# Pairing float32 products of two heads, and new durations in the list schedule of a two-layer hybrid encoder

## The chip, the cores and the metric

The kernel runs on one core of one Trainium2 chip. The time is the device time of one execution in microseconds (us). TensorE is called PE here, its weight loads PEld, VectorE DVE, ScalarE ACT, GpSimd POOL, as the profile names them.

## The reference

The kernel computes a trunk of two layers on 512 tokens of width 1024. Each layer is a half-step SwiGLU feed-forward, a mixing block and a second half-step SwiGLU:

```python
for l in range(DEPTH):
    x = x + 0.5 * swiglu(rms_norm(x, norm_ffn1[l]), ffn1_w_in[l], ffn1_w_out[l])
    h = rms_norm(x, norm_mix[l])
    proj = h @ w_in[l]                      # RWKV-7 | band attention | memory attention
    y_rwkv, v_first = rwkv7_time_mix(p_rwkv, h, ...)
    y_att = chunked_rel_attention(aq, ak, av, att_rel_bias[l])
    y_mem = memory_attention(mq, mk, mv)
    merged = (g_rwkv * (y_rwkv @ w_branch_rwkv[l]) + g_att * (y_att @ w_branch_att[l])
              + g_mem * (y_mem @ w_branch_mem[l]))
    x = x + merged @ w_out[l]
    x = x + 0.5 * swiglu(rms_norm(x, norm_ffn2[l]), ffn2_w_in[l], ffn2_w_out[l])
```

RWKV-7 has 8 heads of 64, with a delta-rule state scan over time; the band attention has 8 heads of 64 and sees all earlier chunks of 64 tokens (512 tokens are 8 chunks, so the band is causal by chunk); the memory attention has 4 heads of 128 over 256 memory tokens.

## The kernel before

**Large products.** All products with weights run in float16 as three terms (high by high, high by low, low by high), each 128 rows by 128 columns by 512 moving columns as a rule. The weights come in float32 by DMA and are split into two float16 halves by ACT and DVE (`load_w`). They fill most of the PE's time: `g<-hh,wh` and its likes in the trace.

**Small products.** The three mixers do their inner products in float32. [...] Heads go in pairs `p` of two heads of 64, one on partitions 0 to 63 and one on partitions 64 to 127 (`H2`; `W2` is the same in the other order), four pairs in a layer.

- `rwkv()` works through the four pairs one after the other. For each pair it computes decay and in-context rate from two products of 64 rows by 128 columns by 512 (`s<-xwa,lw` in the trace; lora products below), then the pair's matrices, a triangular inverse by levels (`each`, 16 products of 64x64x64), and a scan over 8 chunks. In one chunk of the scan the steps depend on each other: the product `xps<-ar,gx`, a copy to `cx`, the product `xps<-cx,tt`, scaled copies to `vu` (`kk` and `ta` in the trace), the product `xps<-kk,kb` and `xps<-ta,be`, and two writes of the next state `z` (`ar<-xps,aw,czc`). The chunk's output `yp` takes four products (two for each head, summed in PSUM), on which nothing in the scan waits.
- `band()` works through the four pairs of attention heads. For each block `b` of 128 queries and each head `u`, `soft(b, u)` makes one score product of 64 rows by 128 columns by `nk` = 128(b+1) keys (`as<-ak,aq`), adds the bias, takes the maximum, exponentials, and scales; `turn` transposes the result into PSUM (`as<-con,sc`) and copies it out (`pt`). Both take their PSUM tile from `a_ps()`, a ring of two banks. `soft` of the next head is called ahead of `turn` of the one before.
- `mem_att()` follows `band()` on the same ring, one of the four memory heads after the other.
- `branch` makes gates and output products for the three mixers, band first, RWKV last. Its sums `acc` lie where the attention's tiles were, so they wait for the end of `mem_att()`.

The lora products, the levels and the transposes of `rwkv()` take PSUM from `s_ps()`, also a ring of two banks.

**What sets the order.** The program isn't issued as written. Recorders note every call with its tiles; `Plan.run` then makes a list schedule: it plays the five engines with estimated durations (`Plan.cost`) and hop times between engines (`HOPS`, `Plan.hop`), takes on each engine the ready operation with the longest path to the end (`key`), and issues the calls in that order. All instructions of PE therefore carry one line, L538, where the calls are made. Operations of a `plan.block()` stay together. For PE, an operation that isn't float16 adds 0.45 of its duration to a debt, and above 0.5 us of debt a float16 product goes first. Where the play finds PE idle for more than 0.4 us it puts in products of zeros (`xps<-wt`) to keep the clock. The estimated PE durations before are these:

```python
if lhs.off.size <= CH // 2:
    return 0.015 + n / 1200
if lhs.off.size <= CH:
    return 0.0255 + n / 1200
return 0.01 + n / 600
```

`n` is the number of moving columns; a block's duration is the sum over its products.

Of the kernel before, what the change touches and what calls it, by code (L numbers as in the profile page):

```python
# [16 lines left out]
P = 128  # L17
# [8 lines left out]
CH = 64  # L26
# [184 lines left out]
class Op:  # L211
    __slots__ = ("eng", "calls", "us", "deps", "succ", "tail", "n", "left", "ready", "end", "bytes", "cols", "big", "phase", "sum", "lift")
# [15 lines left out]
class Plan:  # L228
    HOPS = {"PE": (0.2, 0.2), "S": (0.14, 0.27), "V": (0.14, 0.21), "G": (0.06, 0.3), "D": (0.5, 0.5)}
# [36 lines left out]
    def block(self):  # L266
        plan = self

        class Block:
            def __enter__(s):  # L270
                plan.cur = plan.new("PE")

            def __exit__(s, *a):
                plan.cur = None

        return Block()
# [59 lines left out]
    def cost(self, o, eng, name, out, ins, k):  # L336
# [5 lines left out]
        if eng == "PE":  # L342
            n = out.off.size
            if n <= 2:
                return 0.16
            if name == "transpose":
                o.cols += n
                return 0.005 + n / 1200
            rhs, lhs = k["rhs"], k["lhsT"]
            if rhs.root.dt == F16:  # L350
                o.cols += n
                o.big = True
                o.sum = id(out.root), int(out.off.flat[0])
                return 0.0028 + n / 2400
            o.cols += 2 * n * (rhs.p1 - rhs.p0) / P
            if lhs.off.size <= CH // 2:
                return 0.015 + n / 1200
            if lhs.off.size <= CH:
                return 0.0255 + n / 1200
            return 0.01 + n / 600  # L360
# [3 lines left out]
        if eng == "V":  # L364
            if name == "memset" or name == "reciprocal" and n <= 8:
                return 0.075
            if name in ("tensor_scalar", "tensor_copy") and not psum and out.root.dt != I32:
                return 0.07 + n / 1920 + 0.06 * aps
            return 0.07 + n / 960 + 0.06 * aps
        if eng == "S":  # L370
            return (0.06 if psum else 0.1) + n / 1200 + 0.09 * ((aps > 0) + ("accum_out" in k))
# [168 lines left out]
    def hop(self, a, b):  # L540
# [3 lines left out]
        if a.eng == b.eng:  # L544
            return 0.12 if a.eng == "V" else 0.0
# [10 lines left out]
def trunk(tc: tile.TileContext, i: dict, out: bass.AP, dbg: dict | None = None, depth: int = DEPTH):  # L556
# [414 lines left out]
    def mixing(l, pieces, kst):  # L971
# [106 lines left out]
        def band():  # L1078
            for p in range(NP):
# [22 lines left out]
                def soft(b, u):  # L1102
                    nk = (b + 1) * P
                    h = H2[u]
                    ps = a_ps()
                    PE.matmul(ps[:, :nk], lhsT=q_[h, b * P:(b + 1) * P], rhs=k_[h, 0:nk], start=True, stop=True)
# [23 lines left out]
                for b in range(4):  # L1130
                    for u in range(2):
                        pend.append(soft(b, u))
                        if len(pend) > 1:
                            turn(*pend.pop(0))
# [100 lines left out]
        def rwkv():  # L1235
            for p in range(NP):
# [17 lines left out]
                ps = s_ps()  # L1254
                PE.matmul(ps, lhsT=glob["lw"][0:CH, cs], rhs=glob["xwa"][0:CH, :], start=True, stop=True)
# [3 lines left out]
                ps = s_ps()  # L1259
                PE.matmul(ps, lhsT=glob["lw"][CH:P, cs], rhs=glob["xwa"][CH:P, :], start=True, stop=True)  # L1260
                ta = tr("ta")
                S.activation(ta, ps, AF.Tanh, scale=0.5, bias=lv["a0"][:, p:p + 1])
# [114 lines left out]
                for c in range(NCH):  # L1377
# [26 lines left out]
                    with plan.block():  # L1404
                        for u, h in enumerate(H2):
                            o, w = yp[h, c * CH:(c + 1) * CH], W2[u]
                            PE.matmul(o, lhsT=gx[:, c, u, CH:2 * CH], rhs=vz[:, c, u, :], start=True, stop=False)
                            PE.matmul(o, lhsT=g1[w, c, :], rhs=vu[u][w, c, :], start=False, stop=True)
# [269 lines left out]
```

## Time and profile before

| | |
|---|---|
| median of 3 runs | 2773.04 us (2770.26 to 2778.02) |
| profiled execution, its own time | 2773.73 us |
| its span, first to last instruction | 2771.9 us |
| DVE busy | 1626.2 us (59%) |
| ACT busy | 1538.0 us (55%) |
| granted PE clock, mean | 0.999 of 2.4 GHz |

The profile gives busy time as the union of the intervals of an engine's instructions. For PE these overlap: a float16 product of 512 columns shows some 0.38 us, and the next one starts 0.22 us after it. What a product costs PE is therefore read from the distance between starts (to the start of what follows), not from its own length.

### The profile page before, as it was taken

The numbers are of one execution on the slowest core, as the hardware profiler recorded it, in microseconds if no ns is written. First come the engines' busy times: TensorE is split into PE (matmuls) and PEld (weight loads), VectorE is DVE, ScalarE is ACT, GpSimd is POOL, SyncE is SP. The second block draws the span as 40 slices with busy tenths as digits, with TensorE's granted clock in tenths as the row PEclk, the third lists the DMA queues.
The fourth block names the chain that finished last, engine by engine and source line by source line (L and its number), as shares of the span: only waits on it lengthen the run. The fifth ranks groups of instructions, "written<-read, shape, count | busy, mean of one in ns | idle before, by whom it ended". The sixth has DMA issues, their size and how long they took to land. (4 is left out here: it accounts for less than half of the span.)

```text
span 2771.9 us, 45458 instructions
## 1 busy us (share of the span) xinstructions
PE 2745.1 (99%) x18153; PEld 1496.6 (54%) x18153; DVE 1626.2 (59%) x4391; ACT 1538.0 (55%) x2543; POOL 111.1 (4%) x285
## 2 busy tenths in 40 slices
PE   9999999999999999999999999999999999999999
PEld 6444486565645456444564444765655454654445
DVE  6344486777766676354463544777776666743543
ACT  6556475565645566565455654655655445655652
POOL 0000000000000000000000000000000000000000
PEclk9999999999999999999999999999999999999999
DMA  4222341111121223222222223311212112232332
GB/s 169 105 93 103 122 140 69 51 61 45 52 83 70 85 98 115 95 104 99 99 107 105 93 106 118 129 52 42 70 35 75 67 54 92 92 114 100 107 106 77
DMA packets 47157, 249.36 MB, mean 90 GB/s; under 512 B 5312, under 2 KB 10688, under 8 KB 23648
## 3 DMA queue, kind: packets, MB, share of 16 engines
q1 hardware_dynamic: 46944, 246.45, 25.2%
q8 instruction: 142, 2.33, 0.3%
q14 instruction: 71, 0.58, 0.1%
HBM read 239.09 MB, written 7.34 MB: 89 GB/s over the span
## 5 line engine op out<-in xcount | busy, mean ns | idle before, releaser
L538 PEld LDWEIGHTS <-wh 128*128 128x128 f16 x10920 | 1047.6, 98 | 1008.0 <-issue 26.8
L538 PE MATMUL g<-hh,wh 128*128 128x512 f16 (+1 forms) x3216 | 987.0, 367 | 0.4 <-DVE k L538 0.4
L538 ACT ACTIVATE wh<-wr,qs 128x1024 f16<-128x1024 f32 (+2 forms) x478 | 484.0, 1050 | 222.5 <-PE g L538 114.3
L538 ACT ACTIVATE junk<-wr 128x2048 uint8<-128x2048 f32 (+2 forms) x239 | 412.9, 1727 | 332.9 <-DMA wr<-ffn_in 144.3
L538 PE MATMUL g<-hl,wh 128*128 128x512 f16 (+1 forms) x1608 | 588.9, 366 | 0.0
L538 DVE SCALAR_TENSOR_TENSOR wh<-wr,qs,wh 128x1024 f16<-128x1024 f32 (+2 forms) x478 | 545.2, 1168 | 43.8 <-ACT wh L538 42.9
L538 PE MATMUL as<-hh,wh 128*128 128x512 f16 (+1 forms) x1536 | 443.3, 361 | 0.0
L538 PE MATMUL as<-hl,wh 128*128 128x512 f16 (+1 forms) x768 | 277.4, 361 | 0.0
L538 PE MATMUL as<-ab,wh 128*128 128x512 f16 (+1 forms) x1224 | 234.7, 350 | 0.0
L538 PE MATMUL g<-ab,wh 128*128 128x512 f16 (+1 forms) x1224 | 234.5, 350 | 0.0
L538 POOL PARTITION_ALL_REDUCE ar<-wm x239 | 97.3, 407 | 2465.5 <-ACT junk L538 2313.6
L538 DVE SCALAR_TENSOR_TENSOR a<-as,md,sg 128x512 f32<-128x512 f32 x44 | 33.0, 750 | 213.3 <-PE as L538 210.0
L538 DVE SCALAR_TENSOR_TENSOR a<-g,md,sg 128x512 f32<-128x512 f32 x44 | 33.0, 750 | 212.9 <-PE g L538 202.7
L538 DVE SCALAR_TENSOR_TENSOR x<-g,md,x 128x512 f32<-128x512 f32 (+1 forms) x62 | 39.0, 628 | 115.8 <-PE g L538 115.8
L538 DVE SCALAR_TENSOR_TENSOR x<-as,md,x 128x512 f32<-128x512 f32 (+1 forms) x62 | 38.9, 628 | 115.8 <-PE as L538 115.8
L538 DVE TENSOR_SCALAR qt<-ar 128x1 int32<-128x1 int32 x253 | 37.6, 150 | 104.0 <-POOL ar L538 101.7
L538 ACT ACTIVATE sq<-x 128x256 f32<-128x256 f32 x96 | 37.0, 407 | 78.9 <-DVE x L538 50.6
L538 ACT ACTIVATE kk<-xps 64x64 f32<-64x64 f32 x64 | 14.0, 219 | 112.6 <-DVE ta L538 93.9
L538 ACT ACTIVATE ti<-s 64x256 f32<-64x256 f32 (+1 forms) x144 | 54.3, 378 | 28.2 <-PE s L538 18.3
L538 DVE SCALAR_TENSOR_TENSOR ab<-a,qs,ab 128x512 f16<-128x512 f32 x88 | 60.7, 746 | 10.3 <-ACT ab L538 10.3
L538 ACT ACTIVATE sg<-as,md 128x512 f32<-128x512 f32 x44 | 30.1, 684 | 56.2 <-PE as L538 56.2
L538 ACT ACTIVATE ab<-a,qs 128x512 f16<-128x512 f32 x88 | 55.9, 709 | 7.3 <-DVE qs L538 7.3
(345 smaller groups left out, 3133.4 us busy)
## 6 DMA issues: line engine op xcount, KB each, us to landing
wr<-ffn_in SPq DMA_DIRECT2D x88, 1024.0 KB, 4.8
wr<-ffn_outa SPq DMA_DIRECT2D x32, 1024.0 KB, 4.9
wr<-w_gate SPq DMA_DIRECT2D x24, 1024.0 KB, 4.9
wr<-w_in SPq DMA_DIRECT2D x22, 1024.0 KB, 4.9
wr<-ffn_outb SPq DMA_DIRECT2D x16, 768.0 KB, 4.3
wr<-w_branch SPq DMA_DIRECT2D x24, 512.0 KB, 3.5
wr<-mem_kv SPq DMA_DIRECT2D x8, 1024.0 KB, 4.9
wr<-w_out SPq DMA_DIRECT2D x8, 1024.0 KB, 4.8
```

What stands on the lines that cost most here:

```text
L538: f(*[x.real() if isinstance(x, View) else x for x in a], **{y: x.real() if isinstance(x, View) else x for y, x in k.items()})
```

## The change

The two score products of a block `b` are made together: a new function `scores` takes both banks of the ring and issues both heads' products in one `plan.block()`; `soft` gets its bank as an argument. The two lora products go into one block and take both banks of their ring at once. In the block of `yp` the order of the four products changes from head by head to both first products, then both second ones. In the planner, blocks of 2, 4 or 16 products of given shapes take a duration from the table `GROUPS`; products of up to 2 columns cost 0.2 instead of 0.16; a DVE operation whose input and output start at different partitions costs 0.11 more; and an ACT operation that depends on another of ACT is ready 0.12 us after it instead of at once. What is computed stays the same.

```diff
--- before.py
+++ after.py
@@ -209,7 +209,7 @@
 
 
 class Op:
-    __slots__ = ("eng", "calls", "us", "deps", "succ", "tail", "n", "left", "ready", "end", "bytes", "cols", "big", "phase", "sum", "lift")
+    __slots__ = ("eng", "calls", "us", "deps", "succ", "tail", "n", "left", "ready", "end", "bytes", "cols", "big", "phase", "sum", "lift", "form", "kind")
 
     def __init__(self, eng, n):
         self.eng, self.n = eng, n
@@ -226,6 +226,12 @@
 
 
 class Plan:
+
+    GROUPS = {
+        2: {(128, CH, CH): 0.266, (CH, CH, CH): 0.264, **{(CH, P, n): 0.212 + n * 0.001656 for n in (128, 256, 384, 512)}},
+        4: {(128, CH, CH): 0.5},
+        16: {(CH, CH, CH): 1.08},
+    }
     HOPS = {"PE": (0.2, 0.2), "S": (0.14, 0.27), "V": (0.14, 0.21), "G": (0.06, 0.3), "D": (0.5, 0.5)}
     SLACK = 0.04
     RATIO, DEBT = 0.45, 0.5
@@ -271,6 +277,9 @@
                 plan.cur = plan.new("PE")
 
             def __exit__(s, *a):
+                o = plan.cur
+                if len(o.calls) in plan.GROUPS and o.form in plan.GROUPS[len(o.calls)]:
+                    o.us = plan.GROUPS[len(o.calls)][o.form]
                 plan.cur = None
 
         return Block()
@@ -341,8 +350,9 @@
         n = max([v.off.size for v in ins + [out] if isinstance(v, View)])
         if eng == "PE":
             n = out.off.size
+            o.form = None
             if n <= 2:
-                return 0.16
+                return 0.2
             if name == "transpose":
                 o.cols += n
                 return 0.005 + n / 1200
@@ -353,6 +363,9 @@
                 o.sum = id(out.root), int(out.off.flat[0])
                 return 0.0028 + n / 2400
             o.cols += 2 * n * (rhs.p1 - rhs.p0) / P
+            if len(o.calls) == 1:
+                o.kind = (rhs.p1 - rhs.p0, lhs.off.size, n)
+            o.form = o.kind
             if lhs.off.size <= CH // 2:
                 return 0.015 + n / 1200
             if lhs.off.size <= CH:
@@ -362,11 +375,20 @@
         aps = sum(v.off.size == 1 and v is not out and n > 1 for v in vs)
         psum = any(v.root.pool.kw.get("space") == PSUM for v in ins)
         if eng == "V":
+            moved = 0.11 * bool(ins and isinstance(out, View) and ins[0].p0 != out.p0 and name != "memset")
+            return moved + self.cost_v(name, n, aps, psum, out)
+        return self.cost_s(eng, name, n, aps, psum, k)
+
+    @staticmethod
+    def cost_v(name, n, aps, psum, out):
             if name == "memset" or name == "reciprocal" and n <= 8:
                 return 0.075
             if name in ("tensor_scalar", "tensor_copy") and not psum and out.root.dt != I32:
                 return 0.07 + n / 1920 + 0.06 * aps
             return 0.07 + n / 960 + 0.06 * aps
+
+    @staticmethod
+    def cost_s(eng, name, n, aps, psum, k):
         if eng == "S":
             return (0.06 if psum else 0.1) + n / 1200 + 0.09 * ((aps > 0) + ("accum_out" in k))
         if name == "partition_all_reduce":
@@ -542,7 +564,7 @@
         if a.eng not in self.HOPS:
             return 0.0
         if a.eng == b.eng:
-            return 0.12 if a.eng == "V" else 0.0
+            return 0.12 if a.eng in "VS" else 0.0
         return self.HOPS[a.eng][b.eng == "PE"] + self.SLACK
 
     def key(self, o):
@@ -1099,11 +1121,16 @@
                     t = ta_("pt", [P, 1280], bufs=2)
                     pt.append([t[:, c0:c0 + T - b * P] for b, c0 in enumerate((0, 512, 896, 1152))])
 
-                def soft(b, u):
+                def scores(b):
                     nk = (b + 1) * P
-                    h = H2[u]
-                    ps = a_ps()
-                    PE.matmul(ps[:, :nk], lhsT=q_[h, b * P:(b + 1) * P], rhs=k_[h, 0:nk], start=True, stop=True)
+                    pss = [a_ps(), a_ps()]
+                    with plan.block():
+                        for ps, h in zip(pss, H2):
+                            PE.matmul(ps[:, :nk], lhsT=q_[h, b * P:(b + 1) * P], rhs=k_[h, 0:nk], start=True, stop=True)
+                    return pss
+
+                def soft(b, u, ps):
+                    nk = (b + 1) * P
                     sc = ta_("sc", bufs=3)
                     far = max(0, nk - 2 * P)
                     for c0, c1, bb in ((0, far, bias[:, u, 0:1].to_broadcast([P, far])), (far, nk, bias[:, u, 2 * P - (nk - far):2 * P])):
@@ -1128,8 +1155,9 @@
 
                 pend = []
                 for b in range(4):
+                    pss = scores(b)
                     for u in range(2):
-                        pend.append(soft(b, u))
+                        pend.append(soft(b, u, pss[u]))
                         if len(pend) > 1:
                             turn(*pend.pop(0))
                 turn(*pend.pop(0))
@@ -1251,15 +1279,15 @@
                 else:
                     D.dma_start(out=vfs[p], in_=v_)
 
-                ps = s_ps()
-                PE.matmul(ps, lhsT=glob["lw"][0:CH, cs], rhs=glob["xwa"][0:CH, :], start=True, stop=True)
+                ps, ps2 = s_ps(), s_ps()
+                with plan.block():
+                    PE.matmul(ps, lhsT=glob["lw"][0:CH, cs], rhs=glob["xwa"][0:CH, :], start=True, stop=True)
+                    PE.matmul(ps2, lhsT=glob["lw"][CH:P, cs], rhs=glob["xwa"][CH:P, :], start=True, stop=True)
                 tz = tr("w", bufs=3)
                 S.activation(tz, ps, AF.Tanh, scale=0.5, bias=lv["w0"][:, p:p + 1])
                 V.tensor_scalar(out=tz, in0=tz, scalar1=1.0, scalar2=None, op0=ALU.add)
-                ps = s_ps()
-                PE.matmul(ps, lhsT=glob["lw"][CH:P, cs], rhs=glob["xwa"][CH:P, :], start=True, stop=True)
                 ta = tr("ta")
-                S.activation(ta, ps, AF.Tanh, scale=0.5, bias=lv["a0"][:, p:p + 1])
+                S.activation(ta, ps2, AF.Tanh, scale=0.5, bias=lv["a0"][:, p:p + 1])
                 cu = tr("w", bufs=3)
                 V.tensor_tensor_scan(out=cu, data0=con[:, C_CM:C_CM + T], data1=tz, initial=0.0, op0=ALU.mult, op1=ALU.add)
 
@@ -1402,9 +1430,10 @@
                             else:
                                 S.activation(z, xp_[w, 2 * CH:3 * CH], AF.Copy, scale=aw[w, c:c + 1])
                     with plan.block():
-                        for u, h in enumerate(H2):
-                            o, w = yp[h, c * CH:(c + 1) * CH], W2[u]
+                        ys = [yp[h, c * CH:(c + 1) * CH] for h in H2]
+                        for u, o in enumerate(ys):
                             PE.matmul(o, lhsT=gx[:, c, u, CH:2 * CH], rhs=vz[:, c, u, :], start=True, stop=False)
+                        for u, (o, w) in enumerate(zip(ys, W2)):
                             PE.matmul(o, lhsT=g1[w, c, :], rhs=vu[u][w, c, :], start=False, stop=True)
```

## Rows read from the trace of the kernel before

**Rows 1.** The page's first part: busy us, share of the span and instructions of each engine.

```profile
PE 2745.1 (99%) x18153; PEld 1496.6 (54%) x18153; DVE 1626.2 (59%) x4391; ACT 1538.0 (55%) x2543; POOL 111.1 (4%) x285
```

**Rows 2.** Busy time of each engine by stretch: the mixing of the first layer, that of the second, and the stretches of `mem_att()` in each. Columns: stretch and its length in us, busy us and instructions of each engine, granted clock, DMA share, GB/s.

```profile
400.00:945.00 545.00, 535.72 (x4583) 307.12 (x4582) 384.01 (x1194) 297.99 (x613) 18.73 (x48) 1.00 0.19 64
1765.00:2323.00 558.00, 549.23 (x4630) 311.78 (x4628) 393.49 (x1196) 303.46 (x622) 19.74 (x48) 1.00 0.19 64
690.00:763.00 73.00, 71.37 (x691) 46.04 (x691) 54.00 (x160) 42.77 (x97) 1.71 (x5) 1.00 0.16 54
2055.00:2139.00 84.00, 81.33 (x721) 50.00 (x723) 63.01 (x181) 48.27 (x106) 1.45 (x5) 1.00 0.09 28
```

**Rows 3.** The groups of PE's instructions, with different shapes kept apart. After the count: busy us in all, mean ns of one record, idle us before them. A float32 product is two records.

```profile
L538 PE MATMUL yp<-ar,gx 128*64 128x64 f32 x256 | 40.3, 239 | 0.0
L538 PE MATMUL xps<-ar,gx 128*64 128x64 f32 x256 | 21.5, 246 | 0.0
L538 PE MATMUL yp<-kk,g 64*64 64x64 f32 x128 | 20.8, 242 | 0.0
L538 PE MATMUL yp<-ta,g 64*64 64x64 f32 x128 | 20.8, 242 | 0.0
L538 PE MATMUL xps<-cx,tt 64*64 64x64 f32 x256 | 21.2, 243 | 0.0
L538 PE MATMUL s<-ar,be 64*64 64x128 f32 x256 | 15.9, 273 | 0.1
L538 PE MATMUL as<-ak,aq 64*128 64x512 f32 x32 | 17.9, 640 | 0.3 <-DVE qt L538 0.3
L538 PE MATMUL as<-ak,aq 64*128 64x384 f32 x32 | 14.5, 535 | 0.0
L538 PE MATMUL as<-ak,aq 64*128 64x256 f32 x32 | 11.1, 428 | 0.0
L538 PE MATMUL as<-ak,aq 64*128 64x128 f32 x32 | 3.9, 322 | 0.0
L538 PE MATMUL s<-xwa,lw 64*128 64x512 f32 x32 | 15.7, 639 | 0.7 <-DVE w L538 0.6
```

**Rows 4.** The timeline of PE (start us, length us, what) around two lora products that already stand next to each other (4 records), and around a single one (2 records).

```profile
421.29 0.38 PE L538 MATMUL g<-hh,wh 128*128 128x512 f16 x1
421.60 1.13 PE L538 MATMUL s<-xwa,lw 64*128 64x512 f32 x4
422.67 0.39 PE L538 MATMUL g<-hh,wh 128*128 128x512 f16 x1
...
542.48 0.38 PE L538 MATMUL g<-hh,wh 128*128 128x512 f16 x1
542.78 1.12 PE L538 MATMUL s<-xwa,lw 64*128 64x512 f32 x2
543.84 0.39 PE L538 MATMUL g<-hh,wh 128*128 128x512 f16 x1
```

**Rows 5.** The timeline of PE in one chunk of the last scan of the first layer: the four products of `yp` (8 records), and the next chunk's first two products, which hold both heads.

```profile
904.20 0.28 PE L538 MATMUL yp<-ar,gx 128*64 128x64 f32 x2
904.41 0.33 PE L538 MATMUL yp<-kk,g 64*64 64x64 f32 x2
904.66 0.33 PE L538 MATMUL yp<-ar,gx 128*64 128x64 f32 x2
904.92 0.33 PE L538 MATMUL yp<-ta,g 64*64 64x64 f32 x2
905.18 0.82 PE L538 MATMUL as<-ym,wh 128*128 128x512 f16 x3
905.93 0.34 PE L538 MATMUL xps<-ar,gx 128*64 128x64 f32 x4
906.20 0.82 PE L538 MATMUL as<-ym,wh 128*128 128x512 f16 x3
906.95 0.33 PE L538 MATMUL xps<-cx,tt 64*64 64x64 f32 x4
907.21 0.39 PE L538 MATMUL g<-hh,wh 128*128 128x512 f16 x1
```

**Rows 6.** The timeline of DVE in the same chunk: the two writes of `z` that the product at 905.93 needs.

```profile
904.48 0.58 DVE L538 SCALAR_TENSOR_TENSOR ar<-xps,aw,czc 64x64 f32<-64x64 f32 x2 [0.75 <-ACT junk L538]
```

**Rows 7.** The end of the first layer's RWKV branch: DVE's first and second finished half of `yr`, and PE's first product that reads it.

```profile
932.76 0.75 DVE L538 SCALAR_TENSOR_TENSOR yr<-yr,qs,yr 128x512 f16<-128x512 f32 x1 [0.54 <-ACT yr L538]
...
945.14 0.81 PE L538 MATMUL as<-yr,wh 128*128 128x512 f16 x3
```

**Rows 8.** Two groups of the band attention, of DVE (the bias of a score) and ACT (copies of transposes), with the idle time before them and what ended it.

```profile
L538 DVE SCALAR_TENSOR_TENSOR sc<-as,rq,bias 128x256 f32<-128x256 f32 x64 | 29.5, 478 | 15.2 <-PE as L538 14.5
L538 ACT ACTIVATE pt<-as 128x128 f32<-128x128 f32 x160 | 33.8, 284 | 28.4 <-PE as L538 27.8
```

**Rows 9.** Products of zeros in the second layer's `mem_att()`, as its end comes (PE's timeline).

```profile
2130.90 1.81 PE L538 MATMUL xps<-wt 128*128 128x320 f16 x12 [0.51 <-DVE cx L538]
...
2137.58 0.85 PE L538 MATMUL xps<-wt 128*128 128x320 f16 x5
```

**Rows 10.** First score products of blocks b = 2 and b = 3 in the third pair of the first layer (PE's timeline).

```profile
612.09 0.91 PE L538 MATMUL as<-ak,aq 64*128 64x384 f32 x2
...
617.83 1.12 PE L538 MATMUL as<-ak,aq 64*128 64x512 f32 x2
```

## The prediction, made before the changed kernel was built or run

> **What bounds the kernel now.** I read the engine totals first: PE is busy for 2745.1 of 2771.9 us, DVE and ACT for less than 60% [rows 1]. The span is a sequence of PE instructions with hardly a hole, so a microsecond less of PE's work can be worth a microsecond, provided that no other chain takes over where the work went. Then I cut the span into stages. All that is paired lies in the two mixing stretches, 545 and 558 us long, in which PE is idle for 545.00 - 535.72 = 9.3 and 558.00 - 549.23 = 8.8 us [rows 2]. The feed-forward stretches are float16 products alone, and the change leaves these as they are.
>
> Third, I asked whether a chain beside PE ends at the same moment. In the scan, the second write of `z` ends at 904.48 + 0.58 = 905.06, and the product that needs it starts at 905.93 [rows 5, 6]: the chain waits for PE's queue, not PE for the chain. At the end of the first layer's RWKV branch the first finished half of `yr` is there at 933.5, and PE takes it at 945.14 [rows 7]: 11.6 us of slack. The attention is tighter. Its DVE and ACT groups wait for PE (14.5 of 15.2 us and 27.8 of 28.4 us idle before them [rows 8]), so PE paces it too, but at the end of `mem_att()` PE is fed zeros [rows 9]: there other products have run out, since `acc` waits for the attention's tiles.
>
> **The change part by part.** A float16 product of 512 columns takes 0.216 us of PE, from the starts in [rows 4]. From the last of these to the single lora product at 542.78 are 0.30 us, so going over to float32 costs 0.30 - 0.216 = 0.09 us each time.
>
> *Two lora products in one block.* Alone, one takes 543.84 - 542.78 = 1.06 us, with the entry 1.15. In the first pair of the first layer the schedule put both next to each other by itself: four records in 422.67 - 421.60 = 1.07 us [rows 4]. So the second product is free, and a pair gains 1.06 + 1.06 - 1.07 + 0.09 = 1.14 us. The row's 32 records are 8 pairs; busy 15.7 us [rows 3] is what 6 single pairs (12 x 1.12) and 2 joint ones (2 x 1.13) sum to, so 6 pairs gain: 6.8 us. The block needs both banks at once, which can hold the first product back until the last reader of the other bank is done. I price this at nothing, as the norm of the keys runs beside it; bounds 0 and 2 us for each of 8 pairs.
>
> *Scores of two heads.* Of 128 columns: 32 records in 3.9 us busy, 0.49 a pair, which is one product's length and not two; these stand together already and gain nothing. The others are single: 11.1 / 16 = 0.69, 14.5 / 16 = 0.91 and 17.9 / 16 = 1.12 us of busy time for 256, 384 and 512 columns [rows 3]. The tail that overlaps what follows is 1.12 - 1.06 = 0.06 us, so PE pays 0.63, 0.85 and 1.06. As with lora, a pair should cost what one does; it gains 0.63, 0.85 and 1.06 plus an entry of 0.09 each. Over 4 pairs of heads in 2 layers: 8 x (0.72 + 0.94 + 1.15) = 22.5 us.
>
> *The order of the `yp` products.* The block takes 905.18 - 904.20 = 0.98 us now, in four stretches of 0.21 to 0.26 us [rows 5], each with one head's product alone in the array. Its products side by side are in the trace already: the same shape with both heads takes 906.20 - 905.93 = 0.27 us for `xps<-ar,gx`, and the 64x64 pair takes 907.21 - 906.95 = 0.26 us [rows 5]. So 0.53 instead of 0.98, or 0.50 if the two stretches are as short as those inside the block now; a gain of 0.45 to 0.48, or a little more after a float16 product. I take 0.48. There are 64 blocks (256 + 256 records, 8 each): 30.7 us. The groups say the same from further off: `yp<-ar,gx` is 40.3 us busy where as many records of one shape with `xps` are 21.5 [rows 3].
>
> The Trainium skill speaks against a part of this. "TensorEngine Tiling (Array Packing)", section "Restrictions and Gotchas", says that different row tiles cannot access the same PSUM bank at the same time. The second products of the two heads are such a pair: rows 64 to 127 and 0 to 63, both into `yp`. By the rule they would still take turns, and the `yp` term would be about half. The trace disagrees: `xps<-cx,tt` has two row tiles and one bank and takes 0.26 us for both, and `s<-ar,be`, which goes crosswise into one bank, has 256 records of 128 columns in 15.9 us [rows 3, 5], 0.06 us each.
>
> Together 6.8 + 22.5 + 30.7 = 60.0 us less PE work.
>
> *The planner's new durations.* These change no instruction, only the order. A pair in the scan is now planned at 0.26, as the trace has it, where the old formula gave 2 x (0.0255 + 64 / 1200) = 0.158; the `yp` block goes from 0.315 to 0.5, where the old order really took 0.98; the 16 level products from 1.26 to 1.08. Chain and PE both get longer in the plan by similar sums, so I expect about as many float16 products between two chain steps as now. ACT's 0.12 and DVE's 0.11 make the plan more cautious. Behind a misplaced product everything on PE waits, as it issues in order. Bounds: of the 18.1 us idle and some 6 us of zeros in mixing the plan could win perhaps 12, and as it now overlooks less PE time, which was cover for late DVE and ACT results, it could add about 18, as much as there is now. I take nothing.
>
> **How much of the 60 reaches the end.** From `mem_att()`'s end to the stage's end (763 to 945 and 2139 to 2323) lie two of the four scans and one lora pair per layer: 32 x 0.48 + 2 x 1.14 = 17.7 us. There both slacks above cover it: a `yp` block shorter by 0.48 still leaves 0.87 - 0.48 = 0.39 us between `z` and its reader. I count it in full.
>
> Before it lie 60.0 - 17.7 = 42.3 us. This stretch ends with the attention. If attention shifts forward as PE does, all comes through; if it keeps its pace, nothing does, and PE gets more zeros before 763 and 2139. As [rows 8] show it waiting for PE, and as half of these savings are its own products, I take two thirds: 28 us. Late next is `mem_att()` itself, whose 73 and 84 us no edit shortens.
>
> Sum: 17.7 + 28 = 46 us, against the profiled execution's own 2773.73 us: 2728. That execution lies 0.7 us above the median, so 2727 against the median of 2773.04. If everything comes through 2714, with a better plan 2702.
>
> **The rivals.**
>
> *The `yp` pairs share a bank and take turns.* Half of 30.7 is lost from the gross sum; about 15 us: 2742. The rows above speak against it; for it only that no accumulating pair of this kind is in the trace. (The Trainium skill's rule on row tiles and banks, above, would have it so.) Chance 0.06.
>
> *Attention keeps its pace.* The 42.3 us become idle time and zeros, only the 17.7 us remain: 2756. For it: zeros at 2130.90 and 2137.58 [rows 9] and four memory heads one after the other on two banks. Against it: [rows 8]. Chance 0.15.
>
> *Score pairs make attention slower.* A pair takes both banks of the ring, so `scores(b + 1)` must wait for the copies of `turn(b, 0)`, where a single score waited only for the bias of the one before. Three copies of 0.284 us [rows 8] and the transposes before them make about 1.5 us on each of 3 passages between blocks: 3 x 1.5 x 4 pairs = 18 us per layer. If this lies on the path, PE's savings ahead of it turn to zeros, and the time is 2773.7 + 36 - 17.7 = 2792. It decides from 17.7 / 24 = 0.74 us per passage on. Against it: from the first score of b = 2 to that of b = 3 there are 617.83 - 612.09 = 5.7 us now [rows 10], which is more than one head's bias, exponential and copies need, so the added wait may be over before PE comes to it. Chance 0.11.
>
> *Nothing reaches the end.* The plan spends the freed time on waits: 2771. Chance 0.08.
>
> **How the numbers follow.** The forecast has 0.60, its own range is 2712 to 2742. The range for 8 in 10 takes in its bounds, the shared bank and the unmoved attention with some stall on top: 2702 to 2766; outside are the slower rival, the null case and little below. What this kernel's measurement can tell from no change is about 0.3%, 8 us, so faster means below 2765: 0.60 + 0.06 + 0.15 = 0.81. Same is the null case, 0.08; slower 0.11.
>
> **What would show it right or wrong.** Score records in fours, with 256 to 512 columns at half the busy time of [rows 3]; all lora records in fours; `yp` blocks of about 0.5 us from start to start and `yp<-ar,gx` near 21 us busy. Both mixing stretches shorter by about 23 us each, the feed-forward ones unchanged. If zeros or idle time before the first `g<-ya` products grow by 10 us or more a layer, attention kept its pace. If band attention from its first score to its last product takes longer than now, the slower rival is at work. A `yp` block at 0.75 us would be the shared bank. The prediction is wrong if PE's work falls by 60 us and the time by less than 18, or if the time moves outside mixing.

## The result and the profile after

The changed kernel takes 2737.57 us (median of 4 runs, 2735.70 to 2739.19) beside 2773.94 us for the kernel before in the same comparison. The ratio is 0.9868 with a 95% interval of 0.9851 to 0.9885: 36.4 us less. The forecast was 2727 us. Its profiled execution took 2737.47 us, with a span of 2735.7 us. All calls carry the line L560 now.

The page's first part, engine totals of the changed kernel, to be held against [rows 1]:

```profile
PE 2703.3 (99%) x18240; PEld 1475.1 (54%) x18240; DVE 1629.8 (60%) x4391; ACT 1533.8 (56%) x2543; POOL 109.9 (4%) x285
```

PE is still the bound, with 41.8 us less busy time. But it has more instructions than before, 18240 and not 18153: the zeros. The groups of PE's instructions by shape, as in [rows 3] (count, busy us, mean ns of one):

```profile
L560 PE MATMUL xps<-wt 128*128 128x320 f16 x424 | 67.4, 307 | 3.5 <-DVE ta L560 2.2 <-DVE wt L560 1.0 <-DVE cx L560 0.3
...
L560 PE MATMUL yp<-ar,gx 128*64 128x64 f32 x256 | 19.6, 232 | 0.0
L560 PE MATMUL s<-xwa,lw 64*128 64x512 f32 x32 | 10.4, 641 | 0.0
L560 PE MATMUL as<-ak,aq 64*128 64x512 f32 x32 | 9.0, 641 | 0.0
L560 PE MATMUL as<-ak,aq 64*128 64x384 f32 x32 | 7.3, 535 | 0.0
L560 PE MATMUL as<-ak,aq 64*128 64x256 f32 x32 | 5.6, 428 | 0.0
L560 PE MATMUL as<-ak,aq 64*128 64x128 f32 x32 | 4.0, 329 | 0.6 <-DVE ak L560 0.6
```

Scores of 256 to 512 columns have half the busy time of [rows 3], the lora products two thirds, `yp<-ar,gx` half. The group `xps<-wt` is the products of zeros; before it was this:

```profile
L538 PE MATMUL xps<-wt 128*128 128x320 f16 x337 | 55.5, 315 | 1.8 <-DVE wt L538 1.0 <-DVE cx L538 0.5 <-ACT kk L538 0.3
```

To see where the time went I cut each layer's mixing into a stretch A, from its beginning (the product `s<-con,na` at 356.06 us before and 352.31 after) to the last product of `mem_att()` (`as<-pt,mv`, at 758.91 and 750.83), and a stretch B, from there to the first product of the RWKV branch that reads `yr` (945.14 and 924.05). One sum `g<-ya` of the branches already lies ahead of the end of A (from 740.05 before, from 711.46 after); the write of `acc` behind it is what waits for `mem_att()`. Windows of the kernel before, in the order A, B, the feed-forward stretch between the layers, A, B (length, then busy us and instructions of each engine, clock, DMA share, GB/s):

```profile
356.00:760.00 404.00, 397.69 (x3642) 254.28 (x3640) 307.00 (x1027) 244.88 (x530) 13.35 (x34) 1.00 0.20 69
760.00:945.00 185.00, 181.95 (x1338) 91.54 (x1337) 118.54 (x309) 87.95 (x146) 6.97 (x18) 1.00 0.22 75
945.00:1745.00 800.00, 800.00 (x4239) 414.72 (x4237) 398.44 (x896) 446.21 (x616) 33.38 (x86) 1.00 0.29 103
1745.00:2137.00 392.00, 384.84 (x3440) 237.12 (x3439) 294.69 (x953) 232.55 (x507) 12.92 (x33) 1.00 0.18 60
2137.00:2323.00 186.00, 184.39 (x1372) 92.39 (x1371) 118.08 (x311) 88.76 (x149) 7.97 (x18) 1.00 0.23 82
```

The same windows of the changed kernel:

```profile
352.00:751.00 399.00, 391.55 (x3755) 253.27 (x3753) 313.78 (x1044) 245.81 (x536) 14.53 (x35) 1.00 0.22 76
751.00:924.00 173.00, 169.62 (x1280) 83.99 (x1281) 114.44 (x291) 85.09 (x140) 7.03 (x18) 1.00 0.19 68
924.00:1724.00 800.00, 799.85 (x4233) 414.32 (x4232) 397.95 (x896) 445.75 (x614) 33.21 (x86) 1.00 0.29 103
1724.00:2111.00 387.00, 374.90 (x3518) 233.02 (x3516) 297.57 (x963) 234.83 (x513) 12.24 (x34) 0.99 0.20 69
2111.00:2285.00 174.00, 172.80 (x1331) 85.41 (x1332) 118.97 (x306) 86.83 (x144) 6.27 (x17) 1.00 0.20 69
```

A became shorter by 5 and 5 us, B by 12 and 12, the stretch between by nothing; the mixing starts 4 us earlier and what follows it is 2 us longer (449 and 451 to the end). Sum: 5 + 5 + 12 + 12 + 4 - 2 = 36. The zeros alone, in A of both layers, before and after (length, busy us and count on PE first):

```profile
356.00:760.00 404.00, 5.44 (x36) 3.51 (x36) 0.00 (x0) 1.00 0.20 69
1745.00:2137.00 392.00, 5.46 (x35) 3.43 (x35) 0.00 (x0) 1.00 0.18 60
```

```profile
352.00:751.00 399.00, 14.00 (x91) 8.71 (x91) 0.00 (x0) 1.00 0.22 76
1724.00:2111.00 387.00, 10.77 (x70) 6.76 (x70) 0.00 (x0) 0.99 0.20 69
```

Idle time and zeros in A were 404 - 397.69 + 5.44 = 11.8 us in the first layer and 12.6 in the second; now they are 21.5 and 22.9. So PE's real work in A fell by 14.7 and 15.2 us, and only 5 of each reached the end of the stretch. In B busy time fell by 12.3 and 11.6 us and all of it arrived.

### The profile page after: what moved, and what is told of

It reads as the page before. It is cut to its first block, busy times and chain, and to the rows that moved or that the text cites. A ratio compares the mean times of both kernels' runs of the same rounds, so it can differ in the third digit from the quotient of the medians.

```text
span 2735.7 us, 45594 instructions
## 1 busy us (share of the span) xinstructions
PE 2703.3 (99%) x18240; PEld 1475.1 (54%) x18240; DVE 1629.8 (60%) x4391; ACT 1533.8 (56%) x2543; POOL 109.9 (4%) x285
## 4 chain that ended last, share of the span: by engine, by line
PE 87%; DVE 8%; ACT 3%; DMA 1%; issue 1%; SPq 0%; POOL 0%; ACTq 0%; DVEq 0%; POOLq 0%
PE g L560 45%; PE as L560 33%; PE s L560 5%; PE xps L560 3%; DVE wh L560 1%; PE yp L560 1%; DVE gx L560 1%; ACT wh L560 1%; DVE rs L560 1%; DVE w L560 1%; ACT pt L560 1%; ACT junk L560 0%; DMA wr<-w_in 0%; ACT ti L560 0%; DVE tt L560 0%
## 5 line engine op out<-in xcount | busy, mean ns | idle before, releaser
L560 PEld LDWEIGHTS <-wh 128*128 128x128 f16 x10920 | 1049.6, 98 | 1012.2 <-issue 26.6
L560 PE MATMUL g<-hh,wh 128*128 128x512 f16 (+1 forms) x3216 | 983.7, 367 | 0.9 <-ACT hh L560 0.9
L560 ACT ACTIVATE wh<-wr,qs 128x1024 f16<-128x1024 f32 (+2 forms) x478 | 483.4, 1050 | 233.4 <-PE g L560 125.9
L560 ACT ACTIVATE junk<-wr 128x2048 uint8<-128x2048 f32 (+2 forms) x239 | 412.9, 1727 | 344.0 <-DMA wr<-ffn_in 148.4
L560 PE MATMUL g<-hl,wh 128*128 128x512 f16 (+1 forms) x1608 | 589.4, 367 | 0.3 <-DVE hl L560 0.2
L560 DVE SCALAR_TENSOR_TENSOR wh<-wr,qs,wh 128x1024 f16<-128x1024 f32 (+2 forms) x478 | 544.6, 1168 | 55.3 <-ACT wh L560 54.4
L560 PE MATMUL as<-hh,wh 128*128 128x512 f16 (+1 forms) x1536 | 443.3, 361 | 0.0
L560 PE MATMUL as<-hl,wh 128*128 128x512 f16 (+1 forms) x768 | 277.4, 361 | 0.0
L560 PE MATMUL as<-ab,wh 128*128 128x512 f16 (+1 forms) x1224 | 234.7, 350 | 0.0
L560 PE MATMUL g<-ab,wh 128*128 128x512 f16 (+1 forms) x1224 | 234.5, 350 | 0.0
L560 POOL PARTITION_ALL_REDUCE ar<-wm x239 | 95.6, 400 | 2378.7 <-ACT junk L560 2193.1
L560 DVE SCALAR_TENSOR_TENSOR a<-g,md,sg 128x512 f32<-128x512 f32 x44 | 33.0, 750 | 214.2 <-PE g L560 209.8
L560 DVE SCALAR_TENSOR_TENSOR a<-as,md,sg 128x512 f32<-128x512 f32 x44 | 33.0, 750 | 209.6 <-PE as L560 206.6
L560 DVE SCALAR_TENSOR_TENSOR x<-g,md,x 128x512 f32<-128x512 f32 (+1 forms) x62 | 38.9, 628 | 117.8 <-PE g L560 117.8
L560 DVE SCALAR_TENSOR_TENSOR x<-as,md,x 128x512 f32<-128x512 f32 (+1 forms) x62 | 38.9, 628 | 115.6 <-PE as L560 115.6
L560 DVE TENSOR_SCALAR qt<-ar 128x1 int32<-128x1 int32 x253 | 37.7, 150 | 114.9 <-POOL ar L560 113.0
L560 ACT ACTIVATE sq<-x 128x256 f32<-128x256 f32 x96 | 37.0, 407 | 78.8 <-DVE x L560 51.3
L560 PE MATMUL xps<-wt 128*128 128x320 f16 x424 | 67.4, 307 | 3.5 <-DVE ta L560 2.2
L560 DVE SCALAR_TENSOR_TENSOR ab<-a,qs,ab 128x512 f16<-128x512 f32 x88 | 60.7, 747 | 9.2 <-ACT ab L560 9.1
L560 ACT ACTIVATE ti<-s 64x256 f32<-64x256 f32 (+1 forms) x144 | 54.5, 378 | 15.1 <-PE s L560 9.4
L560 ACT ACTIVATE sg<-as,md 128x512 f32<-128x512 f32 x44 | 30.1, 685 | 56.7 <-PE as L560 56.7
L560 ACT ACTIVATE ab<-a,qs 128x512 f16<-128x512 f32 x88 | 55.9, 709 | 8.4 <-DVE qs L560 8.4
```

The source lines that it names most:

```text
L560: f(*[x.real() if isinstance(x, View) else x for x in a], **{y: x.real() if isinstance(x, View) else x for y, x in k.items()})
```

## The experiments

Medians are given with the ratio to the kernel before, run on the same chip, and its 95% interval. The medians of the kernel before were 2772.7 us for e1 to e4, 2773.3 for e5 to e8 and 2774.0 for e9 to e12.

**Durations and order taken apart (e1, e2).** e1 keeps all pairs and gives the planner its old durations; e2 keeps the old products and gives the planner the new durations, with the `yp` block at the 1.0 us that it takes in the old order [rows 5].

```diff
-                if len(o.calls) in plan.GROUPS and o.form in plan.GROUPS[len(o.calls)]:
+                if False and len(o.calls) in plan.GROUPS and o.form in plan.GROUPS[len(o.calls)]:
...
-                return 0.2
+                return 0.16
...
-            moved = 0.11 * bool(ins and isinstance(out, View) and ins[0].p0 != out.p0 and name != "memset")
+            moved = 0.0 * bool(ins and isinstance(out, View) and ins[0].p0 != out.p0 and name != "memset")
...
-            return 0.12 if a.eng in "VS" else 0.0
+            return 0.12 if a.eng == "V" else 0.0
```

> The paired products stay; the planner plans with all its old durations. Theory A (the freed PE time is lost where float16 products run out beside the attention, and the new durations matter little): 2735 to 2745 us. Rival B (the new durations do a good part of the gain, as an order planned with wrong ones leaves holes): 2752 us or more.

Measured: 2745.86 us, 0.9905 (0.9890 to 0.9919). It lies 1 us above the first of the expected ranges. By this the new durations are worth 8 us beside the pairs; how far a difference of this size can be read, e9 to e12 show.

The main lines of e2, held against the changed kernel:

```diff
-        4: {(128, CH, CH): 0.5},
+        4: {(128, CH, CH): 1.0},
...
-                def soft(b, u, ps):
+                def soft(b, u):
...
-                        ys = [yp[h, c * CH:(c + 1) * CH] for h in H2]
-                        for u, o in enumerate(ys):
+                        for u, h in enumerate(H2):
+                            o, w = yp[h, c * CH:(c + 1) * CH], W2[u]
```

> The products stand as in the kernel before; only the planner's durations are the new ones (the yp block planned at 1.0 us, what it takes in this order). Theory A: the start's 4 us alone come, 2766 to 2774 us. Rival B: 2755 us or less. If the new durations cost time by themselves: over 2780 us.

Measured: 2783.49 us, 1.0041 (1.0026 to 1.0055): 11 us slower than before, in the last of the expected ranges. The same edit to the planner goes with a loss of 11 us with one set of products and with a gain of 8 with the other; part of the 11 can be TensorE's clock (below).

**Scores single again (e3), and the hole that they leave (e4).** e3 is the changed kernel with the old `soft`, which takes one bank for one head.

```diff
-                def soft(b, u, ps):
+                def soft(b, u):
                     nk = (b + 1) * P
+                    h = H2[u]
+                    ps = a_ps()
+                    PE.matmul(ps[:, :nk], lhsT=q_[h, b * P:(b + 1) * P], rhs=k_[h, 0:nk], start=True, stop=True)
...
```

> As the changed kernel, but the scores are made one head at a time again; 22.5 us of PE work come back, all of it ahead of the end of the memory attention. Theory A: this stretch is set by the attention and PE is fed zeros there, so the zeros shrink and the time is 2738 to 2746 us. Theory C (waiting for both banks slows the attention): 2737 us or less. If PE's work counts in full: 2760 us.

Measured: 2738.08 us, 0.9876 (0.9861 to 0.9891), the same as the changed kernel. It lies at the edge between the ranges of theories A and C, so this time alone does not choose between them. The score pairs save 47.4 - 25.9 = 21.5 us of PE's busy time (the four groups of [rows 3] less those after) and bring nothing that shows in the time. The windows of A in e3:

```profile
353.00:750.00 397.00, 393.41 (x3684) 251.56 (x3684) 312.00 (x1038) 245.56 (x534) 14.09 (x34) 1.00 0.20 68
1721.00:2113.00 392.00, 381.76 (x3469) 235.35 (x3469) 295.03 (x957) 233.39 (x511) 11.65 (x33) 0.98 0.18 60
```

Its zeros there are 6.15 and 4.75 us, so idle time and zeros come to 9.7 and 15.0 us, where the pairs have 21.5 and 22.9. What the pairs saved is what PE now stands empty.

One such place is in the last pair of heads of the first layer, here in PE's timeline of the changed kernel (start, length, what):

```profile
655.24 1.95 PE L560 MATMUL xps<-wt 128*128 128x320 f16 x13
657.12 1.97 PE L560 MATMUL s<-xwa,lw 64*128 64x512 f32 x4
...
659.40 1.12 PE L560 MATMUL xps<-wt 128*128 128x320 f16 x7
...
661.24 1.13 PE L560 MATMUL as<-ak,aq 64*128 64x512 f32 x4
662.30 1.55 PE L560 MATMUL xps<-wt 128*128 128x320 f16 x10
663.82 0.38 PE L560 MATMUL g<-hh,wh 128*128 128x512 f16 x1
```

PE has nothing but zeros around the last score pair at 661.24, and 0.8 us after PE has left it (at 662.30) ACT writes the next tiles `aq` and `ak`:

```profile
663.10 0.67 ACT L560 ACTIVATE aq<-g,md 128x512 f32<-128x512 f32 x1
663.67 0.68 ACT L560 ACTIVATE ak<-g,md 128x512 f32<-128x512 f32 x1
```

These belong to the memory queries, whose projections fill PE next and go into the ring of two tiles that the scores read. e4 puts all but the first of these tiles elsewhere.

```diff
-                        t = ta_("ak" if u else "aq", bufs=2)
+                        if p == 0:
+                            t = ta_("ak" if u else "aq", bufs=2)
+                        elif u == 0:
+                            t = ta_("vt", [P, 4, P], bufs=2).rearrange("p b n -> p (b n)")
+                        else:
+                            t = tm("ym", bufs=4)
```

> As the changed kernel, but the last two memory queries are written to other tiles, so that their projection doesn't wait for the last scores of the band attention. In the changed kernel PE gets zeros or nothing for some 5.5 us in each layer there. If this hole is a loss of its own: 2726 to 2731 us. If the attention sets the pace to the end of the memory attention, the zeros only move there: 2735 to 2740 us.

Measured: 2734.72 us, 0.9863 (0.9846 to 0.9879), 2.9 us under the changed kernel, which the intervals don't separate and which is just under the second of the expected ranges. The hole at 655 is gone, which shows its cause, but zeros came back near the end of `mem_att()` (3.9 us from 720 to 740, where the changed kernel has 0.6). In A they are still these:

```profile
355.00:755.00 400.00, 10.73 (x65) 6.45 (x65) 0.00 (x0) 0.99 0.22 75
1726.00:2110.00 384.00, 7.88 (x49) 4.73 (x49) 0.00 (x0) 0.99 0.21 70
```

A is 400 and 384 us long here, beside 399 and 387 after: with the hole filled, the attention ends almost when it ended. The emptiness moved; it did not go.

**The parts alone (e5, e6).** e5 has the new durations and the new `yp` order, with scores and lora products single; it is e2 with the last hunk of the change and the planned 0.5.

```diff
-                ps, ps2 = s_ps(), s_ps()
-                with plan.block():
-                    PE.matmul(ps, lhsT=glob["lw"][0:CH, cs], rhs=glob["xwa"][0:CH, :], start=True, stop=True)
-                    PE.matmul(ps2, lhsT=glob["lw"][CH:P, cs], rhs=glob["xwa"][CH:P, :], start=True, stop=True)
+                ps = s_ps()
+                PE.matmul(ps, lhsT=glob["lw"][0:CH, cs], rhs=glob["xwa"][0:CH, :], start=True, stop=True)
...
```

> New durations and the new order of the yp products; scores and lora products one by one as before. If the yp order carries the gain: 2738 to 2745 us, near the run with single scores. If the lora pairs matter as much: 2748 us or more.

Measured: 2751.53 us, 0.9917 (0.9903 to 0.9932), in the second of the expected ranges. Against e2 that is 32 us, as much as the 30.7 at which the `yp` order was priced. From e5 to e3, which adds the lora pairs, are some 13 us, twice their 6.8. Step by step from the kernel before: durations +11, `yp` order -32, lora pairs -13, score pairs -0.5; sum -35. Each of these steps holds the scatter between orders that e9 to e12 show.

e6 is the changed kernel with `GROUPS` alone of the new durations (the other three lines as in e1).

> The changed kernel with the new durations for groups of products alone; ACT on ACT, DVE across partitions and products of 2 columns are planned as before. If the products' durations make the 8 us between the changed kernel and the run with all old durations: 2735 to 2740 us. If the ACT and DVE terms do: 2743 to 2748 us.

Measured: 2738.15 us, 0.9871 (0.9856 to 0.9886), as with all of them. So the 8 us of e1, as far as they are more than scatter, come from the durations of the products; ACT's 0.12 and DVE's 0.11 bring nothing that shows here.

**The ring of two banks (e7, e8).** In the changed kernel `scores(b)` takes both banks. Between it and `scores(b + 1)` stand `turn(b - 1, 1)` and `turn(b, 0)`, each on one bank; so the next pair waits until the first head's softmax of its own predecessor is done, transposed and copied out. e7 lets `turn` lag by one head more, so that the two turns between pairs are both of block b - 1.

```diff
-                        if len(pend) > 1:
+                        if len(pend) > 2:
                             turn(*pend.pop(0))
                 turn(*pend.pop(0))
+                turn(*pend.pop(0))
```

> As the changed kernel, but the transposes of both heads come one score pair later in the program, so a pair waits for the copies of the block before the last and not for those of the last. Theory C (a score pair's wait for both banks slows the attention, which eats the 22.5 us that pairing frees): 2720 to 2730 us, with the passages between blocks shorter and most zeros gone. If the attention's pace is set by something else: 2735 to 2740 us.

Measured: 2721.89 us (2721.40 to 2722.90), 0.9813 (0.9798 to 0.9828): 15.7 us under the changed kernel, the best version found. The first scores of the four blocks in the last pair of heads of the first layer, PE's timeline of the kernel before, the changed one and e7 in turn:

```profile
654.67 0.49 PE L538 MATMUL as<-ak,aq 64*128 64x128 f32 x4
656.11 0.70 PE L538 MATMUL as<-ak,aq 64*128 64x256 f32 x2
...
664.03 0.91 PE L538 MATMUL as<-ak,aq 64*128 64x384 f32 x2
...
670.98 1.12 PE L538 MATMUL as<-ak,aq 64*128 64x512 f32 x2
```

```profile
639.00 0.49 PE L560 MATMUL as<-ak,aq 64*128 64x128 f32 x4
...
644.24 0.70 PE L560 MATMUL as<-ak,aq 64*128 64x256 f32 x4
...
651.78 0.92 PE L560 MATMUL as<-ak,aq 64*128 64x384 f32 x4
...
661.24 1.13 PE L560 MATMUL as<-ak,aq 64*128 64x512 f32 x4
```

```profile
634.61 0.49 PE L560 MATMUL as<-ak,aq 64*128 64x128 f32 x4
...
637.34 0.70 PE L560 MATMUL as<-ak,aq 64*128 64x256 f32 x4
...
641.59 0.92 PE L560 MATMUL as<-ak,aq 64*128 64x384 f32 x4
...
647.51 1.13 PE L560 MATMUL as<-ak,aq 64*128 64x512 f32 x4
```

From the first block to the last it took 16.3 us before, 22.2 after and 12.9 in e7. From a pair's first score to its first product of `pt` with `vt`, summed over the four pairs, the first and second layer take 161.1 and 160.5 us before, 156.7 and 165.2 after, 149.4 and 156.0 with single scores (e3), 136.5 and 140.3 in e7. So the pairs lengthen the attention by 7 to 9 us a layer against the single scores of e3. (This sum alone does not set the time: e5 has 131.2 and 146.6 us and is 13 us slower than e3.)

The passages from block to block show the wait itself, whatever the order. From the first score of the first block to that of the last, summed over the four pairs of heads, the two layers take 86.5 and 75.5 us before, 112.6 and 105.2 after, 81.2 and 73.1 in e3, 71.9 and 79.1 in e7. In all six kernels with pairs and the old place of `turn` (the changed one, e1, e4, e6, e10, e11) these sums are 103 to 113 us; in all others, with single scores or with pairs and the later `turn`, 69 to 91. The pairs' wait for both banks lengthens the passages, and the later `turn` takes that away. A in e7:

```profile
354.00:751.00 397.00, 387.33 (x3695) 249.69 (x3694) 312.92 (x1045) 245.22 (x536) 13.43 (x35) 0.98 0.22 76
1721.00:2098.00 377.00, 366.60 (x3481) 229.41 (x3479) 294.33 (x964) 234.98 (x514) 12.55 (x34) 1.00 0.21 71
```

In the first layer A is only 2 us shorter than after, in the second 10 us.

e8 makes the same edit to e3, single scores, so that it shows what the later `turn` does without pairs.

> The same later transposes with scores one head at a time. Theory C: a single score never waited for a turn of its own block, so this gains little over single scores alone: 2734 to 2740 us. If the later transposes help by themselves, as much as with pairs: 2728 us or less.

Measured: 2737.70 us, 0.9870 (0.9854 to 0.9887), as e3. The later `turn` alone gives nothing that shows; it is worth something where a pair needs both banks.

**How firm such differences are (e9 to e12).** The planner's order changes everywhere with any duration. These four change only `SLACK`, which is added to each hop between engines, by 0.01 us: in the kernel before, in the changed one (both ways), and in e7.

```diff
-    SLACK = 0.04
+    SLACK = 0.05
```

> The kernel before with a hop between engines planned 0.01 us longer. Nothing else changes but the order that the planner makes. If small differences between orders are noise of some 3 us: 2769 to 2777 us. If any new order moves the time by 8 us or more, the 8 us of the durations and the 11 us that they cost the old products are no property of the durations.

Measured: ratio 1.0020 (1.0010 to 1.0031), 6 us slower: more than the first range allows, less than the 8 us of the other.

> The changed kernel with a hop planned 0.01 us longer. The gain against the kernel before is a property of the change if this is 2733 to 2742 us; an accident of one order if it is 2750 us or more.

Measured: 2735.69 us, 0.9863 (0.9847 to 0.9880), 2 us faster than the changed kernel.

> The changed kernel with a hop planned 0.01 us shorter: 2733 to 2742 us if orders differ by little, else anything from 2725 to 2755 us.

Measured, with 0.03: 2742.69 us, 0.9889 (0.9874 to 0.9904), 5 us slower, just above the first range.

> The version with transposes one score pair later, with a hop planned 0.01 us longer. Theory C (the pair's wait for both banks was what ate the gain): 2717 to 2727 us again. If its 16 us were luck of one order: 2733 us or more.

Measured: 2729.56 us, 0.9839 (0.9824 to 0.9854), 8 us slower than e7 and 6 faster than e10, which has the same slack (their intervals touch). It lies between the two expected ranges, so the size of e7's gain is in part luck of its order: its edit is worth 6 to 16 us, depending on the order it meets. The changed kernel lies 31 to 38 us below the kernel before with all three slacks, so its gain as a whole does not hang on the order. Differences of 5 to 8 us between two orders, as in e1, are no more than this scatter.

**TensorE's clock in these differences.** In the kernel before, the granted clock is full (2.4 GHz) in both mixing stretches [rows 2]. In e9 it falls to half (1.2 GHz) three times (0.50 from 790 to 792 us, for one); these windows of 10 us hold the falls (columns as in [rows 2]):

```profile
790.00:800.00 10.00, 10.00 (x58) 4.25 (x56) 5.06 (x12) 3.74 (x6) 0.00 (x0) 0.84 0.38 126
890.00:900.00 10.00, 10.00 (x61) 4.82 (x59) 6.69 (x14) 3.43 (x6) 0.00 (x0) 0.83 0.30 107
1910.00:1920.00 10.00, 10.00 (x80) 6.33 (x75) 5.93 (x29) 4.02 (x7) 0.00 (x0) 0.83 0.00 0
```

PE is busy there from end to end, and six float16 products take 896.01 - 893.61 = 2.40 us in place of 6 x 0.216 = 1.30. In the changed kernel the clock falls once in mixing, at 538 us, after PE was busy for 1.7 of 4 us. Taking 10 us times one less the clock in each window, an estimate from such rows, the falls cost e9 about 5 us, as much as it is slower; e2 and e3 8.5, e5 and e7 7, e11 5, e10 3, the changed kernel 1.7 and e12 nothing. So most of e2's 11 us can be the clock, single scores (e3) might without it be some us faster than the pairs, and e7 gained its 15.7 us in spite of it, while of the 6 us between e12 and e10 half can be the clock. No run tests this apart. It also moves one and the same kernel: the kernel before took 2770.72 us in an execution with a mean clock of 1.000 and 2777.92 in one with 0.997.

## Why the prediction was right, and which of its steps was not

The time lies inside the range and 10.6 us above the forecast, within the forecast's own range of 2712 to 2742. Faster was the likeliest sign. In part that is luck: A brought 18 us less than the 28 that were counted, while B brought 6 more than its 17.7 and the mixing began 4 us earlier, which no term of its sum held.

*The gross sum of 60 us* holds to about a tenth: PE's busy time less the zeros fell by 41.8 + 11.9 = 53.7 us. (The 0.216 us of a float16 product that it starts from does not stand in [rows 4]; three starts next to each other in the same trace, 737.74, 737.96 and 738.17, show it.) The `yp` block, PE's timeline of the changed kernel:

```profile
638.52 0.29 PE L560 MATMUL yp<-ar,gx 128*64 128x64 f32 x4
638.73 0.27 PE L560 MATMUL yp<-kk,g 64*64 64x64 f32 x1
638.74 0.27 PE L560 MATMUL yp<-ta,g 64*64 64x64 f32 x1
638.84 0.22 PE L560 MATMUL yp<-kk,g 64*64 64x64 f32 x1
638.85 0.22 PE L560 MATMUL yp<-ta,g 64*64 64x64 f32 x1
639.00 0.49 PE L560 MATMUL as<-ak,aq 64*128 64x128 f32 x4
```

It takes 639.00 - 638.52 = 0.48 us, as priced, where [rows 5] had 0.98. Of the 56 blocks that the timeline shows apart, 55 take 0.47 to 0.53 us; before, 49 such blocks took 0.98 to 1.03. A score pair costs its one product's length, as priced. The lora products lost 5.3 us busy; one of the eight pairs, at 657.12 above, takes 1.97 us and not 1.13, which is within the 0 to 2 us that the prediction allowed a pair for the wait for both banks. That wait is in the trace: the weights of its second product are loaded only at 657.96, when DVE's `yr<-w,pv,s`, which reads a tile of the same ring, has ended (657.17 + 0.74).

*The shared bank* did not happen. `yp<-kk,g` and `yp<-ta,g` lie on different rows of the array and write crosswise into the two halves of one bank's partitions, both adding to it, and start 0.01 us apart. The rule of the Trainium skill ("TensorEngine Tiling (Array Packing)", section "Restrictions and Gotchas"), by which different row tiles cannot access one PSUM bank at the same time, isn't borne out by this trace: 0.48 us a block, where turns would have made about 0.75. Two row tiles that write into the same partitions of a bank were not tried.

*Behind the attention the saving arrives in full.* B gave 24 us. The term was 17.7; PE's busy time in B fell by 23.9 us, more than its own pairs save, as some work moved ahead into A: B has 58 and 40 records fewer than before, though the change takes no product away.

*Ahead of the attention's end two thirds arrive.* This step failed: of the 42.3 us, 29.9 showed up as less work in A and 10 arrived, in place of 28. Idle time and zeros in A grew by 9.7 and 10.3 us, close to the 10 us a layer that the prediction had named as the sign of the attention keeping its pace. (It named the first `g<-ya` as the end of that stretch; here it is the end of `mem_att()`.) The prediction had counted the attention's own products as a reason why their savings would come through. It is the other way round: e3 shows that just these 22.5 us bring nothing, while the rest of the change, which is e3, lies 34.6 us under the kernel before, of the 60.0 - 22.5 = 37.5 us at which the `yp` order and the lora pairs were priced. What took the scores' saving away is the pairs' wait for both banks: with it moved back (e7), A in both layers is 22 us shorter than before.

*The third rival* had the mechanism, at a chance of 0.11, and put its price beside the sum instead of against the scores' own term. It priced a passage between blocks at 1.5 us; the twelve of a layer grew by 26 and 30 us, 2.2 and 2.5 each. Its argument against itself, that the 5.7 us of [rows 10] hold more than a softmax needs, took the length of a passage for its slack. The pairs made three passages longer by 5.9 us together in the pair shown, and the attention as a whole longer than with the single scores of e3, but in sum no longer than before (-4.4 and +4.7 us). So the loss about cancelled the gain, and no more.

*The planner's durations at nothing*: +11 us with the old products, -8 with the new, inside the bounds of -12 and +18. As the slack shows, 6 us come from order alone, so that these are settled no better than that; so is why the lora pairs seem to give twice their price. Also open is what keeps A of the first layer at 397 us in e7, where the attention is 20 us shorter than after. The time goes in `mem_att()`: the products `as<-pt,vt` of the last pair start 12.8 us earlier than after (660.77 and 673.54), but from there to the last `as<-pt,mv` it takes 89 us and not 77, the end of it at half the clock.

## What to carry to other kernels

Where two products are put side by side, count the buffers that they need at the same moment: a pair that takes a whole ring waits for the last user of every slot, and the loop around it must run one step further ahead before the pair pays. Savings off the chain that sets a stretch's end can come through whole, and savings inside it be lost in the wait that they bring. To judge an edit of a few us in a kernel with a computed order, first see what a change of the planner's constants that means nothing does, and read the granted clock of each execution beside its time.

## What was not expected

0.01 us on each planned hop between engines moves the time by 2 to 8 us (e9 to e12), as much as some parts of this change are worth. Nothing in the executed program differs but the order of its calls and the number of zeros that the planner puts between them (e9 has 18185 PE records, the kernel before 18153). Part of the difference goes with the granted clock, which a new order can let fall.
